# A softmax that streams through SBUF: twelve-row tiles in four buffers in place of eight-row tiles in six

## The chip, the cores and the metric

The kernel runs on one core of one Trainium2 chip, with the chip's other cores idle. The metric is the device time of one execution in microseconds, the median of several runs. Profiled spans are about 1.7 us shorter than timed runs, because a span reaches only from the first instruction to the last. DVE, ACT, POOL and SP are the profile's names for VectorE, ScalarE, GpSimd and SyncE; the first two compute here, and SP, ACT and POOL issue the transfers between memory and SBUF that the 16 DMA engines carry out. A packet is one piece of a transfer on one DMA engine, and its record in the trace has a start, an end and a size.

## The reference

```python
batch, seq, dim = 32, 512, 1024            # x: float32, 67.11 MB
scaled  = x / temperature                  # temperature = 0.5
shifted = scaled - np.max(scaled, axis=-1, keepdims=True)
exp_x   = np.exp(shifted)
return exp_x / np.sum(exp_x, axis=-1, keepdims=True)
```

That is a softmax over 16,384 rows of 1,024 numbers. Every byte is read once and written once, and each row is independent of the others.

## The kernel before

The 16,384 rows are 128 rows for each of 128 partitions. A tile holds 8 rows a partition (4.19 MB), there are 16 tiles, and 6 buffers hold them in turn. A "row" below is one row on each of 128 partitions, 0.524 MB.

```python
ROWS = 8
BUFS = 6
PASSES = [[4, 4]] * 2 + [[8]] * 12 + [[4, 4]] * 2    # rows of each pass over a tile
WHOLE = (2, 4, 6, 8, 10, 12)                         # tiles multiplied by one instruction a pass
ALONE = 14
# ...
def dram(t, i):                 # partition p holds rows p*8 .. p*8+7: 32 KB that lie together
    block = t[P * ROWS * i : P * ROWS * (i + 1), :]
    return block.rearrange("(p k) d -> p k d", p=P, k=ROWS)
```

SP issues the loads. For a pass g of k rows of tile i, DVE takes the maxima, and ACT the exponentials with their sums. DVE then divides, either row by row or as one multiplication by a second tensor:

```python
nc.vector.reciprocal(recip, sums)
if i in WHOLE:
    xt = tiles[i][:, a : a + k, :]
    nc.vector.tensor_mul(xt, xt, recip.unsqueeze(2).to_broadcast([P, k, d]))
    return
for b in range(k):
    nc.vector.tensor_scalar_mul(
        tiles[i][:, a + b, :], in0=tiles[i][:, a + b, :], scalar1=recip[:, b : b + 1])
```

ACT issues the stores, and each store's end frees the buffer for a later load. One row of tile 0 is stored early from GpSimd. The loop divides a pass after it has taken the maxima of the next one, except that the first pass of the last tiles (from ALONE on) lets the division go first:

```python
for _ in range(BUFS):
    load()
for g in range(len(groups) + 1):
    alone = g < len(groups) and groups[g][0] >= ALONE and groups[g][1] == 0
    if g > 0 and alone:
        divide(g - 1); store(g - 1)        # store: a tile's last pass stores it and calls load()
    if g < len(groups):
        maximum(g); exponential(g)
    if g > 0 and not alone:
        divide(g - 1); store(g - 1)
```

Of the kernel before, what the change touches and what calls it, by code (L numbers as in the profile page):

```python
# [1 line left out]

# [4 lines left out]



ROWS = 8  # L10
BUFS = 6

PASSES = [[4, 4]] * 2 + [[8]] * 12 + [[4, 4]] * 2

WHOLE = (2, 4, 6, 8, 10, 12)

ALONE = 14


@with_exitstack  # L20
def kernel(
    ctx: ExitStack,
    tc: tile.TileContext,
    x: bass.AP,
    temperature: bass.AP,
    out: bass.AP,
):
    nc = tc.nc
    f32 = mybir.dt.float32
    scale = 1.0 / float(temperature)  # L30
    extreme = mybir.AluOpType.max if scale > 0 else mybir.AluOpType.min

    P = 128
    xf = x.flatten_outer_dims()
    of = out.flatten_outer_dims()
    n, d = xf.shape
    assert len(PASSES) * ROWS * P == n

    data = ctx.enter_context(tc.tile_pool(name="data", bufs=BUFS))
    stats = ctx.enter_context(tc.tile_pool(name="stats", bufs=4))  # L40


    groups = []
    for i, ks in enumerate(PASSES):
        assert sum(ks) == ROWS
        for j, k in enumerate(ks):
            groups.append((i, sum(ks[:j]), k))

    def dram(t, i):
        block = t[P * ROWS * i : P * ROWS * (i + 1), :]  # L50
        return block.rearrange("(p k) d -> p k d", p=P, k=ROWS)

    tiles, small = [], []

    def load():
        i = len(tiles)
        if i < len(PASSES):
            xt = data.tile([P, ROWS, d], f32, name="xt")
            nc.sync.dma_start(out=xt, in_=dram(xf, i))
            tiles.append(xt)  # L60

    def maximum(g):
        i, a, k = groups[g]
        top, bias, sums, recip = (
            stats.tile([P, k], f32, name=name) for name in ("top", "bias", "sums", "recip")
        )
        small.append((bias, sums, recip))
        nc.vector.tensor_reduce(  # L68
            out=top, in_=tiles[i][:, a : a + k, :], axis=mybir.AxisListType.X, op=extreme
        )  # L70
        nc.vector.tensor_scalar_mul(bias, in0=top, scalar1=-scale)  # L71

    def exponential(g):
        i, a, k = groups[g]
        bias, sums, _ = small[g]
        for b in range(k):
            nc.scalar.activation(  # L77
                tiles[i][:, a + b, :],
                tiles[i][:, a + b, :],
                mybir.ActivationFunctionType.Exp,  # L80
                bias=bias[:, b : b + 1],
                scale=scale,
                accum_out=sums[:, b : b + 1],
            )

    def divide(g):
        i, a, k = groups[g]
        _, sums, recip = small[g]
# [7 lines that stand above are left out]
                tiles[i][:, a + b, :], in0=tiles[i][:, a + b, :], scalar1=recip[:, b : b + 1]  # L96
            )

    def store(g):
        i, a, k = groups[g]  # L100


        if g == 0:
            nc.gpsimd.dma_start(out=dram(of, i)[:, :1, :], in_=tiles[i][:, :1, :])  # L104
        elif a + k == ROWS:
            a = 1 if i == 0 else 0
            nc.scalar.dma_start(out=dram(of, i)[:, a:, :], in_=tiles[i][:, a:, :])
            load()



    with tc.manual_schedule():
# [6 lines that stand above are left out]
                divide(g - 1)  # L119
                store(g - 1)  # L120
            if g < len(groups):
                maximum(g)
                exponential(g)
            if g > 0 and not alone:
                divide(g - 1)
                store(g - 1)


# [1 line left out]
_INS = ['x', 'temperature']  # L130
_OUTS = [((32, 512, 1024), 'float32')]

_NUMBERS = {'temperature': 0.5}


# [26 lines left out]
```

## Time and profile before

| | before |
|---|---|
| time, median of the first 3 runs | 317.21 us |
| profiled span | 315.7 us |
| DVE busy | 251.0 us (79%) |
| ACT busy | 148.1 us (47%) |
| DMA queues, share of 16 engines' span | 99.0% |
| bytes in and out | 134.2 MB, 425 GB/s |

How to read it: no engine that computes is full, while the 16 DMA engines are. Their share averages over the whole span, so the rows by slice and stretch that the prediction shows are needed to see that no stage differs. SP's long waits for stores, and DVE's for loads, are what a full transfer path looks like from the engines' side.

### The profile page before, as it was taken

What the parts mean: (1) busy time and instruction counts of PE and PEld (TensorE: products, weight loads), DVE (VectorE), ACT (ScalarE), POOL (GpSimd) and SP (SyncE); (2) the same over time, 40 slices, a digit from 0 to 9 for tenths busy, and PEclk for the clock granted to TensorE, in tenths of its full rate; (3) what the DMA queues carried; (4) which work ended last, traced back from release to release, by engine and by line L of the source; (5) the groups of instructions that cost most, each with busy time, mean ns of one, the idle gap of its engine ahead of it and who ended that gap; (6) DMA issues with size and microseconds to landing.
All of it is one profiled execution on the core that took longest, in us unless ns stands there. A gap on an engine that the chain in (4) does not pass through costs nothing. (4 is left out here: it accounts for less than half of the span.)

```text
span 315.7 us, 534 instructions
## 1 busy us (share of the span) xinstructions
DVE 251.0 (79%) x146; ACT 148.1 (47%) x257; POOL 1.3 (0%) x5
## 2 busy tenths in 40 slices
DVE  0399999999679795897949979399793999979710
ACT  0176637680906519074290833808247091564700
POOL 0001000000000000000000000000000000000000
DMA  8999999999999999999999999999999999999996
GB/s 328 415 448 421 369 441 434 465 400 461 404 457 407 457 411 457 428 436 436 428 448 415 448 415 449 411 465 403 461 403 461 403 461 403 461 403 461 407 457 274
DMA packets 4755, 134.24 MB, mean 425 GB/s; under 512 B 528, under 2 KB 528, under 8 KB 656
## 3 DMA queue, kind: packets, MB, share of 16 engines
q1 hardware_dynamic: 2304, 67.11, 49.7%
q10 hardware_dynamic: 2304, 66.59, 48.9%
q0 software_dynamic: 144, 0.52, 0.4%
q14 instruction: 3, 0.02, 0.0%
HBM read 67.11 MB, written 67.11 MB: 425 GB/s over the span
## 5 line engine op out<-in xcount | busy, mean ns | idle before, releaser
L77 ACT ACTIVATE xt<-xt,bias 128x1024 f32<-128x1024 f32 x128 | 145.2, 1135 | 136.6 <-DVE bias L71 127.1
L68 DVE TENSOR_REDUCE top<-xt 128x8 f32<-128x8192 f32 (+1 forms) x20 | 139.5, 6976 | 44.4 <-DMA xt<-in_x_dram 44.4
L95 DVE TENSOR_SCALAR xt<-xt,recip 128x1024 f32<-128x1024 f32 x80 | 54.3, 748 | 0.5
L92 DVE TENSOR_TENSOR xt<-xt,recip 128x8192 f32<-128x8192 f32 x6 | 52.2, 8692 | 0.2
L77 ACT ACTIVATION_READ_ACCUMULATOR xt<-xt,bias 128x1 f32 x128 | 23.9, 187 | 0.0
L77 ACT ACT_TABLE_LOAD x1 | 1.3, 1283 | 13.3 <-DMA xt<-in_x_dram 13.3
L89 DVE RECIPROCAL recip<-sums 128x8 f32<-128x8 f32 (+1 forms) x20 | 3.8, 188 | 4.1 <-ACT xt L77 4.1
L71 DVE TENSOR_SCALAR bias<-top 128x8 f32<-128x8 f32 (+1 forms) x20 | 3.4, 171 | 0.7
L104 POOL DMA_DIRECT2D out_dram<-xt x1 | 1.1, 1142 | 23.4 <-DVE xt L95 23.4
L143 POOL MEMSET const-bfloat16-1.0<- 128x1 bf16 x1 | 0.1, 96 | 0.0
L143 POOL MEMSET const-float32-0.0<- 128x1 f32 x1 | 0.1, 93 | 0.2 <-issue 0.2
L143 POOL MEMSET const-float32-1.0<- 128x1 f32 x1 | 0.1, 93 | 0.0
L143 POOL MEMSET const-uint8-127<- 128x1 uint8 x1 | 0.1, 93 | 0.0
## 6 DMA issues: line engine op xcount, KB each, us to landing
xt<-in_x_dram SPq DMA_DIRECT2D x16, 4096.0 KB, 51.2
out_dram<-xt ACTq DMA_DIRECT2D x15, 4096.0 KB, 28.0
out_dram<-xt ACTq DMA_DIRECT2D x1, 3584.0 KB, 23.2
out_dram<-xt POOLq DMA_DIRECT2D x1, 512.0 KB, 19.6
```

What stands on the lines that cost most here:

```text
L68: nc.vector.tensor_reduce(out=top, in_=tiles[i][:, a : a + k, :], axis=mybir.AxisListType.X, op=extreme)
L71: nc.vector.tensor_scalar_mul(bias, in0=top, scalar1=-scale)
L77: nc.scalar.activation(tiles[i][:, a + b, :], tiles[i][:, a + b, :], mybir.ActivationFunctionType.Exp, bias=bias[:, b : b + 1], scale=scal ...
L89: nc.vector.reciprocal(recip, sums)
L92: nc.vector.tensor_mul(xt, xt, recip.unsqueeze(2).to_broadcast([P, k, d]))
L95: nc.vector.tensor_scalar_mul(tiles[i][:, a + b, :], in0=tiles[i][:, a + b, :], scalar1=recip[:, b : b + 1])
L104: nc.gpsimd.dma_start(out=dram(of, i)[:, :1, :], in_=tiles[i][:, :1, :])
L143: nc = _bacc.Bacc("TRN2", target_bir_lowering=False, num_devices=1)
```

## The change

The intent: fewer and larger transfers, with the same bytes of SBUF in use (4 x 12 rows in place of 6 x 8). To keep a store from coming too late, a twelve-row tile is worked in two passes of six rows. A one-column copy is put ahead of the first large store on ACT. It reads tile 2 and so makes that store wait until tile 2 has landed.

```diff
-ROWS = 8
-BUFS = 6
+PASSES = [[4, 4, 4]] + [[6, 6]] * 9 + [[4, 4]]
+BUFS = 4
-PASSES = [[4, 4]] * 2 + [[8]] * 12 + [[4, 4]] * 2
-WHOLE = (2, 4, 6, 8, 10, 12)
+WHOLE = (2, 3, 4, 6, 8)
-ALONE = 14
+ALONE = 9
 ...
-    block = t[P * ROWS * i : P * ROWS * (i + 1), :]
-    return block.rearrange("(p k) d -> p k d", p=P, k=ROWS)
+    block = t[P * sum(rows[:i]) : P * sum(rows[: i + 1]), :]
+    return block.rearrange("(p k) d -> p k d", p=P, k=rows[i])
 ...
         nc.gpsimd.dma_start(out=dram(of, i)[:, :1, :], in_=tiles[i][:, :1, :])
-    elif a + k == ROWS:
+    elif a + k == rows[i]:
         a = 1 if i == 0 else 0
+        if i == 0:
+            nc.scalar.copy(stats.tile([P, 1], f32, name="seen"), tiles[2][:, 0, 0:1])
         nc.scalar.dma_start(out=dram(of, i)[:, a:, :], in_=tiles[i][:, a:, :])
         load()
```

More of the change, by code (lines that the diff above doesn't have):

```diff
@@ L36 @@
     n, d = xf.shape
-    assert len(PASSES) * ROWS * P == n
+    rows = [sum(ks) for ks in PASSES]
+    assert sum(rows) * P == n
     data = ctx.enter_context(tc.tile_pool(name="data", bufs=BUFS))
@@ L44 @@
     for i, ks in enumerate(PASSES):
-        assert sum(ks) == ROWS
         for j, k in enumerate(ks):
@@ L57, in load @@
         if i < len(PASSES):
-            xt = data.tile([P, ROWS, d], f32, name="xt")
+            xt = data.tile([P, rows[i], d], f32, name="xt")
             nc.sync.dma_start(out=xt, in_=dram(xf, i))
```

## The prediction

> **What bounds the kernel now.** I read the page's shares first, then the DMA rows and queues, the stretches by stage, the waits and the groups.
>
> ```profile
> span 315.7 us, 534 instructions
> DVE 251.0 (79%) x146; ACT 148.1 (47%) x257; POOL 1.3 (0%) x5
> ...
> DMA  8999999999999999999999999999999999999996
> ...
> DMA packets 4755, 134.24 MB, mean 425 GB/s; under 512 B 528, under 2 KB 528, under 8 KB 656
> ...
> q1 hardware_dynamic: 2304, 67.11, 49.7%
> q10 hardware_dynamic: 2304, 66.59, 48.9%
> q0 software_dynamic: 144, 0.52, 0.4%
> ```
>
> No compute engine is full. The DMA row shows 9 in every slice but the first and the last, and the queue shares (loads q1, stores q10, one early store q0) add to 99.0% of 16 engines' span. The stretches say the same, stage by stage (columns: stretch, DVE, ACT, POOL, clock, DMA share, GB/s):
>
> ```profile
> 2.00:34.00 32.00, 20.43 (x17) 14.39 (x24) 1.14 (x1) 1.00 0.99 422
> 34.00:66.00 32.00, 31.79 (x18) 19.69 (x35) 0.00 (x0) 1.00 0.99 419
> ...
> 226.00:290.00 64.00, 56.57 (x41) 28.75 (x51) 0.00 (x0) 1.00 1.01 434
> 290.00:312.00 22.00, 9.02 (x12) 7.95 (x14) 0.00 (x0) 1.00 1.00 430
> 312.00:316.00 4.00, 0.00 (x0) 0.00 (x0) 0.00 (x0) 1.00 0.31 131
> ```
>
> The reader is to see that loads alone (2 to 34 us), both directions (226 to 290) and stores alone (290 to 312) all run at about 430 GB/s. Bytes in either direction cost the same, so the time is all bytes over one rate, plus a head before the first packet and an end after the last. The packet records of the trace put the first data packet at 1.8 us and the last end at 314.5, and between 2 and 313 us 16 packets are under way at once, one for each DMA engine.
>
> ```profile
> DVE top L68 <- DMA xt<-in_x_dram: 44.4, 10, 13.2
> ...
> SPq L59 <- DMA out_dram<-xt: 214.3, 10, 42.9
> ```
>
> DVE waits 44.4 us for loads, and SP waits 214 us for stores to land before it may issue the next load. Both are the shape of a ring of buffers behind a full DMA. The chain that ended last names only the final DVE and ACT work (ACT 6%, DVE 6%), because it doesn't follow transfers. I don't read a bound from it.
>
> ```profile
> L77 ACT ACTIVATE xt<-xt,bias 128x1024 f32<-128x1024 f32 x128 | 145.2, 1135 | 136.6 <-DVE bias L71 127.1 <-issue 9.6
> L68 DVE TENSOR_REDUCE top<-xt 128x8 f32<-128x8192 f32 x12 | 104.2, 8684 | 31.2 <-DMA xt<-in_x_dram 31.2
> L95 DVE TENSOR_SCALAR xt<-xt,recip 128x1024 f32<-128x1024 f32 x80 | 54.3, 748 | 0.5
> L92 DVE TENSOR_TENSOR xt<-xt,recip 128x8192 f32<-128x8192 f32 x6 | 52.2, 8692 | 0.2
> L68 DVE TENSOR_REDUCE top<-xt 128x4 f32<-128x4096 f32 x8 | 35.3, 4412 | 13.2 <-DMA xt<-in_x_dram 13.2
> ```
>
> These are the durations for the working below: a reduce takes 1.085 us a row, an exponential 1.13, a whole multiply 1.087. ACT's idle time comes from waiting on DVE's maxima, DVE's from loads.
>
> **What the Trainium skill says.** "DMA: Bandwidth & Descriptors", section "Where 436 GB/s comes from", gives a ceiling of 435.2 GB/s from 16 ports. The stage rates of 419 to 434 agree: there is almost nothing above them. The same page, "Queues, rings and completion order", says each DMA engine takes turns between queues, a packet at a time. The near-equal shares of q1 and q10 and the records, where 32 KB packets of both alternate, agree. "SBUF — State Buffer", "The DMA setup-cost knee", counts about 2 us fixed for a transfer, mostly completion. Here that cost doesn't show between transfers, since another is always queued; only the head and the end pay it. "VectorE: DVE Perf Modes", "Mode 2×_2P", says a multiply by a per-partition scalar gets two elements a cycle in f32 and one by a second tensor doesn't. The trace agrees: eight scalar multiplies of one row take 5.39 us in the timeline, one 8-row TENSOR_TENSOR 8.69.
>
> **The change part by part.**
>
> (1) Bytes. They stay at 67.11 MB each way. In the records a 32 KB packet takes 1.213 us, a 28 KB one 1.062 and a 4 KB one 0.159. So 4 KB costs 0.151 us and a packet about 0.005 beside it (1.213 - 8 x 0.151). I assume that a partition's 48 KB goes as one packet, as its 32 KB does now; estimate 12 x 0.151 + 0.005 = 1.817 us. Per DMA engine, before: loads 16 x 8 x 1.213 = 155.26; stores 15 x 8 x 1.213 + 8 x 1.062 + 8 x 0.159 = 155.33. After: loads 10 x 8 x 1.817 + 8 x 1.213 = 155.06; stores 8 x (11 x 0.151 + 0.005) + 8 x 0.159 + 9 x 8 x 1.817 + 8 x 1.213 = 155.12. That saves 0.4 us, and ten fewer transfers' closing packets of 0.009 us in each direction 0.2 more at most: 0.5 us together, all on the path.
>
> (2) DVE. Reduces cost 1.085 us a row as now, so 6 rows take 6.5. A whole multiply of 6 rows takes 6.5, six scalar ones 4.06 (5.39 x 6/8). Five tiles by whole passes are 60 rows against 48: (60 - 48) x (1.087 - 0.674) = +5 us in step time (+4 in the busy column, where a scalar row counts 0.748), and three more passes' small instructions +1. DVE busy should be 256 to 262 us (about 82%), still below the DMA. None of it is on the path while stores stay queued.
>
> (3) Order and buffers. 4 x 12 rows are as many bytes of SBUF as 6 x 8. What could go wrong is that both queues run dry, so I laid the schedule out by hand: a row costs 1.213 us of DMA, 12 rows 14.55; with both queues active each takes 29.1.
> - Start: tile 0 lands 4.85 us later than now, at 13.2 + 4.85 = 18.1. Three passes of 4 rows follow the present timeline: divide 0 ends at 30.3, divide 1 at 37.7. The reduce of tile 1's first half then ends at 44.2 and divide 2 at 47.3. The added copy holds the store of tile 0 until tile 2 has landed, at about 3.5 + 3 x 14.55 + 1.2 = 48.4. The loads already issued last until 60, longer with sharing, so nothing idles.
> - Tile 1 is ready for its store at 69, and the store of tile 0 drains at about 75. Tile 2 is ready at 96 against 101, tile 3 at 123 against 130, tile 4 at 151 against 159.
> - Steady: a tile costs DVE 2 x (6.9 + 6.6) = 27 us with whole passes, 22 with scalar ones, against 29.1 of DMA. DVE waits for loads 2 to 7 us a tile, and each store is ready 8 to 11 us before the one ahead of it drains. A store's landing gives its buffer to a load some 3 us before the load queue is empty; were it later, the stores would run alone at the full rate.
> - End: loads finish at about 272. Tile 9 lands at 254, its store is ready at 281, and the store of tile 8 drains at 289. The last tile's at 297, against 303 for tile 9's. The last store then runs 9.7 us to 313. Slack at the end is about 6 us; now it is about 3 (issue at 301.0, its first byte due at 313.5 - 9.7 = 303.8).
>
> Sum: 317.2 - 0.5 + 0 = 316.7 us.
>
> **The rivals.** (A) The queues run dry after all. Tiles are coarser, the store waits for the next tile's first pass, and the added copy holds up ACT's queue. For it: between buffers there are only four steps rather than six. Against it: 6 to 11 us of slack everywhere above. With one or two gaps of 2 to 3 us, 319 to 322. (B) DVE becomes the bound: 27 us a tile against 29.1 leaves only 2 us in whole-pass tiles. Were passes slower by a tenth, tiles 2 to 4 would run late by 0.6 us each and the queued stores would absorb it: no change, or +1. (C) Larger packets aren't neutral. If 48 KB is cut in two, packets cost 0.2 us more in each direction and the gain goes. If the DMA engines end more unevenly, the tail grows: now most end at 313.3 and one at 314.5, and a 48 KB packet more or less on one engine is 1.8 us. 317 to 318.5. (D) More gain than counted: in the records some 45 packets at 34 to 37 us, where the first large store joins the loads, took about 0.4 us too long (45 x 0.4 / 16 = 1.1 us per engine). Holding the store back may spare that: 315.6.
>
> **Range and chances.** C and D pull about equally, A is the only route to a large loss. A range of 315.6 to 318.3 holds C and D alone. Faster by over 2% would need 310.9 us, less than the packet time of 310.4 plus head and end of 3 to 5 us: excluded unless packets themselves get faster, so 0.01. Slower by over 2% is 323.5, which needs 7 us of idle DMA: 0.03.
>
> **What would show it right or wrong.** Right: DMA row all 9 between first and last slice, 425 to 427 GB/s, about 3,315 packets (23 transfers of 144 each, as 33 make 4,752 of the 4,755 now), DVE 256 to 262 us, tile 0's first reduce at 18, the last store issued near 297 and landing some 17 us later, a shorter wait of DVE for loads. Wrong: a slice of the DMA row below 9 in the middle (A), DVE with no wait for loads after tile 4 (B), over 4,500 packets or an end more than 2 us after the rest (C), a rate above 428 GB/s (D).

## The result

| | before | changed |
|---|---|---|
| median of 6 runs | 317.25 us (317.17 to 318.36) | 317.59 us (317.37 to 319.0) |
| profiled span | 315.7 us | 315.6 us |
| DVE busy | 251.0 us | 256.9 us |
| packets | 4,755 | 3,315 |

The ratio is 1.001, with a 95% interval of 0.9988 to 1.0032: the same.

The page of the changed kernel:

```profile
span 315.6 us, 513 instructions
DVE 256.9 (81%) x147; ACT 148.4 (47%) x258; POOL 1.3 (0%) x5
...
DMA  8999999999999999999999999999999999999996
...
DMA packets 3315, 134.24 MB, mean 425 GB/s; under 512 B 368, under 2 KB 368, under 8 KB 496
...
q1 hardware_dynamic: 1584, 67.11, 49.7%
q10 hardware_dynamic: 1584, 66.59, 48.7%
```

There are 1,440 fewer packets, yet the DMA row is digit for digit that of the kernel before and the mean rate is 425 GB/s in both. The stretches of the changed kernel (same columns as in the prediction) tell the same:

```profile
2.00:34.00 32.00, 15.46 (x10) 10.45 (x17) 1.15 (x1) 1.00 0.98 420
34.00:66.00 32.00, 31.72 (x28) 19.43 (x34) 0.00 (x0) 1.00 1.00 419
...
226.00:290.00 64.00, 59.87 (x36) 30.13 (x53) 0.00 (x0) 1.00 1.00 434
290.00:312.00 22.00, 7.65 (x12) 6.52 (x12) 0.00 (x0) 1.00 1.00 431
312.00:316.00 4.00, 0.00 (x0) 0.00 (x0) 0.00 (x0) 1.00 0.15 66
```

Stage by stage the rates differ from those before by at most 2 GB/s. The last stretch looks like a gain and is hardly one: a view counts a packet where it starts, and longer packets start earlier before their end. Shared out over the time of each packet, 0.59 MB moved after 312 us, against 0.64 MB before. The waits and the groups of the changed kernel:

```profile
DVE top L66 <- DMA xt<-in_x_dram: 35.8, 6, 18.3
...
SPq L57 <- DMA out_dram<-xt: 227.3, 7, 59.0
```

```profile
L66 DVE TENSOR_REDUCE top<-xt 128x6 f32<-128x6144 f32 x18 | 117.9, 6547 | 17.5 <-DMA xt<-in_x_dram 17.5
L90 DVE TENSOR_TENSOR xt<-xt,recip 128x6144 f32<-128x6144 f32 x10 | 65.6, 6559 | 0.6 <-DVE recip L87 0.3
L93 DVE TENSOR_SCALAR xt<-xt,recip 128x1024 f32<-128x1024 f32 x68 | 46.2, 748 | 0.5
```

DVE has 5.9 us more to do and waits 8.6 us less for loads. That is work put into a wait, and costs nothing. Where did the packets' time go? Here are sums over the trace's packet records, for one DMA engine on average. "Overlap" is the time in which more than 16 records are open at once, because a packet's record begins some ns before the record ahead of it ends:

```
                                     before    changed
sum of all packet records, us        312.70    312.16
overlap of records, us                 1.04      0.68
time with the DMA engine busy, us    313.27    313.10   (last end less idle time after the
                                                         first data packet: the head before
                                                         it is counted in)
first data packet, us                  1.77      1.75
last data packet ends, us            314.49    314.25
```

The records shrank by 0.54 us, which is the prediction's 0.5. But 0.36 us of it had been overlap already, so an engine was busy only 0.17 us less (313.27 to 313.10; without the head, records less overlap, 311.66 to 311.48). The span shrank by 0.1 us, and the timed runs not at all.

### The profile page after: what moved, and what is told of

Its sections match the earlier page's. It is cut to its first block, busy times and chain, and to the rows that moved or that the text cites. A ratio compares the mean times of both kernels' runs of the same rounds, so it can differ in the third digit from the quotient of the medians.

```text
span 315.6 us, 513 instructions
## 1 busy us (share of the span) xinstructions
DVE 256.9 (81%) x147; ACT 148.4 (47%) x258; POOL 1.3 (0%) x5
## 2 busy tenths in 40 slices
DMA packets 3315, 134.24 MB, mean 425 GB/s; under 512 B 368, under 2 KB 368, under 8 KB 496
## 4 chain that ended last, share of the span: by engine, by line
DMA 51%; DVE 29%; ACT 14%; issue 0%; DVEq 0%; SPq 0%
DMA xt<-in_x_dram 29%; DMA out_dram<-xt 22%; DVE top L66 19%; ACT xt L75 14%; DVE xt L93 7%; DVE xt L90 2%; DVE bias L69 1%; DVE recip L87 0%; DVEq L159 0%; SPq L57 0%
## 5 line engine op out<-in xcount | busy, mean ns | idle before, releaser
L66 DVE TENSOR_REDUCE top<-xt 128x6 f32<-128x6144 f32 (+1 forms) x23 | 139.9, 6084 | 35.8 <-DMA xt<-in_x_dram 35.8
L90 DVE TENSOR_TENSOR xt<-xt,recip 128x6144 f32<-128x6144 f32 x10 | 65.6, 6559 | 0.6 <-DVE recip L87 0.3
L93 DVE TENSOR_SCALAR xt<-xt,recip 128x1024 f32<-128x1024 f32 x68 | 46.2, 748 | 0.5
L87 DVE RECIPROCAL recip<-sums 128x6 f32<-128x6 f32 (+1 forms) x23 | 4.2, 182 | 5.0 <-ACT xt L75 5.0
L69 DVE TENSOR_SCALAR bias<-top 128x6 f32<-128x6 f32 (+1 forms) x23 | 3.9, 171 | 0.8
## 6 DMA issues: line engine op xcount, KB each, us to landing
out_dram<-xt ACTq DMA_DIRECT2D x9, 6144.0 KB, 35.8
```

What stands on the lines that cost most here:

```text
L66: nc.vector.tensor_reduce(out=top, in_=tiles[i][:, a : a + k, :], axis=mybir.AxisListType.X, op=extreme)
L69: nc.vector.tensor_scalar_mul(bias, in0=top, scalar1=-scale)
L93: nc.vector.tensor_scalar_mul(tiles[i][:, a + b, :], in0=tiles[i][:, a + b, :], scalar1=recip[:, b : b + 1])
```

## The experiments

The kernel before ran beside each set as its own reference, so sets on different chips compare by their ratios. The control is the changed kernel itself.

| run | median us | ratio to before (95%) | DVE busy us |
|---|---|---|---|
| control (changed kernel) | 317.72 | 1.0012 (0.9999 to 1.0024) | 256.9 |
| copy only | 318.38 | 1.0030 (1.001 to 1.005) | 0 |
| packets of 4 KB | 326.35 | 1.0281 (1.0265 to 1.0296) | 256.9 |
| no whole passes | 318.18 | 1.0022 (1.0005 to 1.0039) | 232.0 |
| all tiles whole | 324.38 | 1.0218 (1.0203 to 1.0233) | 284.9 |
| tiles 2 to 8 whole | 318.29 | 1.0026 (1.0012 to 1.0041) | 266.8 |
| no copy on ACT | 318.96 | 1.0057 (1.0042 to 1.0072) | 256.9 |
| copy that holds nothing | 319.25 | 1.0058 (1.0037 to 1.008) | 256.9 |
| passes of 12 rows | 335.33 | 1.0566 (1.0548 to 1.0584) | 252.9 |
| three buffers of 12 | 353.59 | 1.1169 (1.1125 to 1.1213) | 257.1 |
| before with four buffers of 8 | 328.05 | 1.0329 (1.0308 to 1.0351) | 251.1 |

### The changed kernel again

No edit; five rounds.

> The changed kernel once more, unaltered, for more rounds. Theory (packet time is equal on the wall): 317.2 to 317.8, ratio to the kernel before 1.000 to 1.002. Prediction: 316.7, ratio 0.998.

Measured 317.72 us (317.31 to 318.04) and a ratio of 1.0012. The interval leaves out the predicted 0.998: the saving of 0.5 us isn't there, and the changed kernel is equal or slower by a tenth of a per cent.

### Transfers alone

```diff
-                maximum(g)
-                exponential(g)
-                divide(g - 1)      (in both places)
```

> The changed kernel with the maxima, exponentials and multiplies left out (its output is x itself, wrong on purpose): the same loads and stores in the same sizes. Theory (the transfers alone set the time of both kernels): it takes as long as the changed kernel, 316.5 to 318, though DVE and ACT do nothing. Rival (some of the time is waits of transfers for compute, or the late start of stores at 48.6 us): 2 us or more faster, 315 or less.

Its output is wrong, which doesn't matter for the time. Measured 318.38 us. The page's engines and DMA row:

```profile
ACT 1.5 (0%) x2; POOL 0.9 (0%) x5
...
DMA  8999999999999999999999999999999999999994
```

DVE does not appear at all, and the time doesn't fall. So no wait for compute is seen in the time of the changed kernel, and nothing suggests that a faster DVE or ACT could shorten it. This run keeps the copy that holds the first large store (issued at 48.75 us here), so it can't tell what the late start of the stores costs; the kernel before issues that store at 32.9 us and takes as long. The run is even some 0.6 us above the control: in the execution profiled, the slowest of four, one DMA engine finished at 316.0 us, while fifteen had finished by 314.3. In its trace the time of a busy DMA engine is 313.09 us, that of the changed kernel 313.10.

### The cost of a packet

```diff
-        return block.rearrange("(p k) d -> p k d", p=P, k=rows[i])
+        return block.rearrange("(k p) d -> p k d", p=P, k=rows[i])
```

> The changed kernel with the rows of a tile dealt to partitions in the other order, so that a partition's run in memory is one row and packets are 4 KB in place of 48 KB; the result stays right. Prediction's step 1 took the whole record of a packet as time on the path: 2 x 1,024 packets of 0.159 us per DMA engine is 325.6 us against 310.4, so +15 us, about 332. Theory now (the records of following packets overlap by about 3.4 ns, so that much of a packet's own cost is hidden): 8 - 3.4 ns on 2,048 packets is +9 us, about 327. Rival (a packet's own cost is wholly hidden): 317 to 318.

```profile
DMA  7999999999999999999999999999999999999997
...
DMA packets 33139, 134.24 MB, mean 414 GB/s; under 512 B 368, under 2 KB 368, under 8 KB 33136
```

Measured 326.35 us, 8.6 above the control. The packet records rose by 15.7 us per DMA engine over the control's (312.29 to 327.94; the prediction's arithmetic gives 15.2), and their overlap rose by 7.0 (0.68 to 7.72). The difference, 8.6, is what the wall saw. That is an account and no test, as records less overlap plus idle time always make up the time; the test is that +9 was written down first. A data packet therefore costs 8.6 us / (2,048 - 184) = 4.6 ns of wall time at 4 KB, not the 8 ns of its record. The overlap theory had +9, the record theory +15 and the hidden one 0, so this run settles it. The edit also changes the order in which rows lie in memory; its packets' records are as long (median 0.159 us) as those of the 4 KB packets of the kernel before, so no effect of the order is seen.

The 4.6 ns are a net figure. When the first large store joins the loads, the changed kernel falls from about 430 GB/s to 313 for 2 us (52 to 54 us, each packet shared out over its time), which is the slow packets that rival D of the prediction names, 0.8 us per DMA engine. With 4 KB packets there is no dip: 410 GB/s before the store joins, 417 as it does, 422 after. Put back, the 0.8 us make about 5 ns a packet (estimate: 9.4 us / 1,864).

### Whole passes: none, all, and the middle ones

```diff
-WHOLE = (2, 3, 4, 6, 8)
+WHOLE = ()                         # no whole passes
+WHOLE = tuple(range(11))           # all
+WHOLE = (2, 3, 4, 5, 6, 7, 8)      # the middle
```

> The changed kernel with no tile multiplied by whole passes. Theory: DVE falls by 60 rows x 0.41 us = 25 us to about 233 us and its wait for loads grows; the time stays within 0.3 us of the changed kernel's, as multiplies are off the path. Rival (the five whole-pass tiles pace the stores so that loads come in time, and are worth something): slower by 1 us or more.

Measured 318.18 us. DVE lost 25 us of work as expected, and the time did not fall. The ratio is 0.001 above the control's, within both intervals: too little to tell, and the rival's 1 us isn't seen. No run here shows what the slower whole passes are good for.

> The changed kernel with all eleven tiles multiplied by whole passes. Theory: 68 rows more at 0.41 us make DVE 285 us or so, 90% of the span; the stores are ready some 5 us later than now in tiles 5, 7, 9 against slack of 6 to 11 us, so the time stays within 0.5 us. Rival (DVE is nearly the bound: 27 us a tile against 29.1): the queues run dry in places, +2 us or more.

Measured 324.38 us: the theory missed and the rival was right about the size, though not about the place. Two stretches of the run with all tiles whole:

```profile
74.00:78.00 4.00, 4.00 (x1) 4.00 (x7) 0.00 (x0) 1.00 0.42 182
...
306.00:310.00 4.00, 4.00 (x1) 0.00 (x0) 0.00 (x0) 1.00 0.40 172
```

The transfers run out twice, at the start and at the end. The expectation had reckoned with the slack of tiles 5, 7 and 9 and forgot that tiles 0, 1 and 10 had become slower as well. The store of tile 1 came at 79.4 us in place of 69.2, where the prediction's schedule gave it 6 us of slack (in the changed kernel it had 7.7, as tile 0's store drained at 76.9); the last store came at 310.2 in place of 299.5. Idle time, the mean over the DMA engines, is 4.4 us above the changed kernel's. Slow packets, those whose records are longer than is usual for their size, cost 2.2 us more: together the 6.7 us measured.

> The changed kernel with tiles 2 to 8 all multiplied by whole passes, the first two and the last two as in the changed kernel. With all eleven whole, DMA idled at 76 to 79 us (the store of tile 1 came 10 us later than in the changed kernel) and at 306 to 310 (the last store 11 us later), 5.2 us in all, with some 2 us of slow packets beside. Theory (slack is short only at the start and the end; in the middle a tile costs DVE 27 us against 29.1): DVE about 267 us, no idle DMA, time within 0.5 us of the changed kernel. Rival (a slower DVE costs time anywhere): +1.5 us or more.

Measured 318.29 us, 0.0014 of 317 = 0.4 us above the control by ratio, with DVE at 266.8 us and no idle DMA between 10 and 310 us. So in the middle DVE has room for 10 us of work more, and at the ends, where all tiles whole ran dry, it has not. The changed kernel's five whole tiles lie inside that room.

### The copy on ACT

```diff
             if i == 0:
-                nc.scalar.copy(stats.tile([P, 1], f32, name="seen"), tiles[2][:, 0, 0:1])
```

> The changed kernel without the added one-column copy on ACT, which holds the first large store until tile 2 has landed. Theory: the store of tile 0 is issued at about 47.4 us in place of 48.6, the loads queued go on, and the time stays within 0.3 us. The slow packets at about 50 us (0.8 us per DMA engine) come with the first large store and move to about 48. Rival (the copy spares the loads a collision): slower by 0.5 us or more, with tile 2 landing later.

Measured 318.96 us and a ratio of 1.0057 against the control's 1.0012 on the same chip; the intervals are apart. The store of tile 0 moved from 48.6 to 47.6 us as expected, but the time rose by 1.2 us, so "within 0.3" missed. The rival had the size, but not its reason: tile 2 landed at 48.2 us against 48.0. The other edit keeps the instruction and removes the hold:

```diff
-                nc.scalar.copy(stats.tile([P, 1], f32, name="seen"), tiles[2][:, 0, 0:1])
+                nc.scalar.copy(stats.tile([P, 1], f32, name="seen"), tiles[1][:, 0, 0:1])
```

> The changed kernel with its added copy reading tile 1, which landed long before, in place of tile 2: the instruction stays, the hold on the first store goes. Theory (the hold is what is worth 1.4 us, by keeping the first large store from joining before tile 2 has landed): store at about 47.5 us and a ratio like that without the copy, 1.004 to 1.007. Rival (the copy's instruction, or chance, made the difference): ratio as of the control, 1.000 to 1.002.

Measured 1.0058, with the store at 47.5 us: the hold is what counts, not the instruction. How it counts is not seen. In these two traces, though not in these alone, the DMA engines part company at the end. I chained the packet records engine by engine, by which packet begins as another ends, and took the time at which each engine finished its last packet. Each row is one execution, and for copy only, no whole passes and tiles 2 to 8 whole it was the slowest of four:

```
                         engines ending      last engine
                         after 314.0 us      ends, us
before                         2               314.49
changed                        1               314.25
control                        3               314.46
no copy on ACT                 4               315.18
copy that holds nothing        7               317.00
copy only                      2               316.02
no whole passes                7               315.16
tiles 2 to 8 whole             3               316.20
```

The mean busy time of an engine, reckoned as above, is alike in all eight (313.09 to 313.67 us), while the last one to finish sets the time: each of these executions took about 3 us more than its last engine's end (2.95 to 3.23). By these chains, in the run whose copy holds nothing, the last engine moved as many bytes as the others, but its records were 5.5 us longer than the medians of their sizes, against 1.5 to 1.9 for the three that ended first. Why its packets were slow when the first large store started 1 us earlier, before tile 2 had landed, stays open. So does why the last three rows have stragglers with the hold in place.

### Less room: longer passes, fewer buffers

```diff
-PASSES = [[4, 4, 4]] + [[6, 6]] * 9 + [[4, 4]]
+PASSES = [[4, 4, 4]] + [[12]] * 9 + [[4, 4]]
```

> The changed kernel with passes of twelve rows in place of two of six. A store then waits for a reduce of 13.1 us in place of 6.5 and for its whole tile's multiply (8.1 or 13.1 us): ready about 10 to 13 us later, against slack of 8 to 11 us. Theory: the store queue runs empty for a few us a tile, but loads fill in until the end; the tail grows, 318 to 322. Rival (the ring of four buffers has room for it): within 0.3 us.

Measured 335.33 us, far above the range of the theory, and its rival is out. Two of its stretches:

```profile
296.00:300.00 4.00, 3.74 (x7) 0.20 (x2) 0.00 (x0) 1.00 0.00 0
300.00:304.00 4.00, 4.00 (x7) 0.00 (x0) 0.00 (x0) 1.00 0.00 0
```

For 8 us nothing moves at all. DVE waits for the twelve exponentials of tile 9 until 296.2, then multiplies twelve rows, and the store is issued at 304.6 in place of 282.8. The end is where the coarse pass costs: idle time rises by 12.7 us and slow packets by 5.0. With four buffers, splitting the pass is thus what keeps the twelve-row tile from costing time.

```diff
-BUFS = 4
+BUFS = 3
```

> The changed kernel with three buffers of twelve rows in place of four. Theory (the change is neutral only because 48 rows in flight leave slack): 36 rows are loaded by 47 us, the first store comes at 48.6, so about 3 us idle there, then loads wait for stores and some gaps follow: 320 to 330, with slices of the DMA row below 9. Rival (even 36 rows cover it): within 1 us.

```profile
DMA  8999969899899988997999799979979999994968
```

Measured 353.59 us. The row dips about every 33 us, once a tile. Idle time rose by 22.6 us and slow packets by 13.2, which add up to the 35.9 us over the control. I had expected gaps, but much smaller ones.

```diff
-BUFS = 6        (in the kernel before)
+BUFS = 4
```

> The kernel before with four buffers of eight rows in place of six: 32 rows in flight, fewer than the 36 that cost the changed kernel 36 us in three buffers. Theory (what counts beside bytes is how many steps there are between buffers; a tile's ring time is 4 x 19.4 = 78 us against 34 from landing to store, 19 for the store, 3 for the handover and 19 for the load = 75): close to covered, 317 to 327. Rival (bytes in flight decide): slower than the 353 of 36 rows.

Measured 328.05 us, 1 us above the range. The rival is out: 32 rows in four steps lose 11 us, 36 rows in three steps 36. So bytes in flight alone do not decide. That the number of steps does is argued and not shown: a tile holds its buffer until its own store ends and waits for its neighbour's pass, but the two runs differ in the size of tiles and passes too. The loss has an odd form. Here are two stretches of this run and then the same of the kernel before (same columns):

```profile
110.00:120.00 10.00, 8.32 (x2) 1.93 (x4) 0.00 (x0) 1.00 1.01 383
...
190.00:200.00 10.00, 8.36 (x2) 3.53 (x8) 0.00 (x0) 1.00 1.00 360
```

```profile
110.00:120.00 10.00, 9.93 (x8) 2.91 (x5) 0.00 (x0) 1.00 1.02 442
...
190.00:200.00 10.00, 9.93 (x11) 5.46 (x9) 0.00 (x0) 1.00 1.00 430
```

With four buffers the DMA engines are as busy as before, but move 383 and 360 GB/s. Their packets take longer. Over the run idle time rose by only 2.2 us against the kernel before, slow packets by 8.4.

The packet records tell which packets are slow. Between 112 and 119 us, 33 load packets are at least 0.1 us longer than the 1.213 us usual for 32 KB, 1.2 us per DMA engine in all, and in that time the stores start again (115.6 us) after 6.3 us without a packet. The same happens at 152, 192, 232 and 273 us, each time where stores start again after 6.3 to 7.9 us. These five make 6.8 of the 8.4 us. Where it is the loads that start again beside running stores, after 5.9 to 7.0 us, no such stretch of slow packets follows (four times, the first at 139.7 us):

```profile
112.00:118.00 6.00, 4.75 (x1) 0.00 (x0) 0.00 (x0) 1.00 0.99 339
...
136.00:144.00 8.00, 7.93 (x4) 0.75 (x1) 0.00 (x0) 1.00 1.04 446
```

## Why the prediction was right or wrong

**The bound: right.** The transfers alone take as long as the kernel (copy only, 318.38 us), and 25 us less DVE work does not shorten it.

**Step 1, bytes: wrong, and it is the step that failed.** It said of the 0.5 us: "all on the path". The packet records did shrink by 0.54 us, so 48 KB packets were assumed rightly (1.815 us measured, 1.817 estimated). But a record isn't wall time: neighbours overlap by some 3.5 ns, and an engine's busy time fell by 0.17 us only. The 4 KB run measures it directly, 8.6 us where the records say 15.7. What was left is below the spread of the last engine's end. One term was also miscounted without effect: ten fewer transfers are five in each direction, which saves 0.09 us and not 0.2. The time lay in the range, 317.59 against 316.7, but the sign of the small difference was not found. That the range held is in part luck: it is 2.7 us wide, five times the effect that was forecast.

**Step 2, DVE: right.** 256.9 us against 256 to 262, and waits 35.8 us against 44.4. The "two elements a cycle" that the prediction cites holds here in direction only: the scalar form was 8.69 / 5.39 = 1.6 times as fast, not twice.

**Step 3, order: right, the stores to within 3 us.** From the timeline of the changed kernel:

```profile
48.55 0.37 ACTq L109 DMA_DIRECT2D out_dram<-xt  x1
51.45 0.17 ACT L108 COPY seen<-xt 128x1 f32<-128x1 f32 x1
...
69.21 0.34 ACTq L109 DMA_DIRECT2D out_dram<-xt  x1
...
95.97 0.34 ACTq L109 DMA_DIRECT2D out_dram<-xt  x1
```

The stores were set down for 48.4, 69 and 96 us, and that of tile 9 and the last for 281 and 297; these came at 282.8 and 299.5; the loads finished at 277 us, not 272. The copy itself runs 2.9 us after the store that it holds back: the wait for tile 2 is in ACT's queue, ahead of the store, while the work stands behind earlier exponentials. No slice of the DMA row is below 9 in the middle. The schedule does not mention that the load queue would run empty for 9 us before 81 us. Its sentence "were it later, the stores would run alone at the full rate" covers it and was right: 431 to 434 GB/s in that pause. What it has no word for is the other side. Where stores start again beside running loads, and where both had stopped, packets were slow: 8 us of them with four buffers, 13 with three.

**The rivals.** A (queues run dry) didn't happen here, and the slack was real: passes of 12, three buffers and all tiles whole each used it up and lost 7 to 36 us. The slack at the two ends was about the 6 us told (7.7 at tile 1's store, 5.0 at the last), so the 10 us of lateness with all tiles whole went past it and cost 6.7. B (DVE as bound) is refuted for the middle tiles by 266.8 us of DVE at no clear cost. C was half right: packets of 48 KB weren't split, but the uneven end of the DMA engines is about the size of the small differences here. D was wrong: the slow packets at the first large store only moved, from 34 to 39 us to 51 to 55, with 0.8 us per engine. With 4 KB packets they were absent.

## What to carry to other kernels

Where all DMA engines are busy from the first slice to the last at one rate, fewer and larger transfers can win only the packets' own cost, and that is to be taken from what the wall sees and not from a sum of records. In this kernel larger tiles were safe only while the ring kept four buffers and the passes stayed short, and the first and last tiles ran out of slack before the middle ones. Look also for a store queue that runs empty and starts again: in the four-buffer run that cost the loads 1.2 to 1.6 us per DMA engine five times over, while the engines counted as busy. A copy-only version of a kernel is the cheapest way to learn whether there is anything left to win.

## What the Trainium skill lacked or had wrong

- "SBUF — State Buffer", "Summary: rules for kernel authors", says to estimate HBM transfers at about 358 GB/s. It leaves out what "HBM Reference", "Specifications (TRN2)", says of this figure: it holds with both cores of a pair streaming, while a core alone gets about 425. The one core here moved 425 GB/s over the whole span, in and out together, so the second page agrees and the rule misleads.
- "DMA: Bandwidth & Descriptors", "Why small descriptors are slow (HBM only)", gives a fixed cost per packet of about 3 cycles, with 256 bytes as its example. It lacks a figure for large packets, and that records overlap. Here a 4 KB packet cost 4.6 ns of wall time while its record shows 8, and 48 KB in place of 32 KB won 0.17 us in 313.
- None of the pages that I read has it that loads slow down when stores start again beside them: with four buffers of 8 rows the kernel lost 8.4 us to slower packets and only 2.2 to idle DMA engines. The reverse doesn't show it: the changed kernel's loads paused for 9 us before 81 us without a slow packet. The 4 KB run shows no dip when its stores start. The cause is open.
- "DMA: Bandwidth & Descriptors", "Latency and other measured facts", says that DMA engines 7 and 15 are usually slower, but not by how much the last engine ends after the rest with equal bytes: in the copy-only run fifteen ended by 314.3 us and the last at 316.0. The packed trace doesn't number the engines, so whether the last is one of those two is open.
